# Weight splits as own programs, memory projections one pass earlier, and buffers lent between stages, in a one-core hybrid attention layer

## The chip, the core and the metric

The kernel runs on one core of a Trainium2 chip. Its time is device time in microseconds (us), the median of several runs. Five engines matter: TensorE (PE in the rows; PEld is its weight load), VectorE (DVE), ScalarE (ACT), GpSimd (POOL) and SyncE (SP), which issues every DMA here from one queue, in order.

## The reference, cut to what matters

One decoder layer over 2048 tokens of width 1024: a normalised input `h`, one wide projection, three groups of heads, gates, an output projection.

```python
h = rmsnorm(x, pre_g)
proj = h @ w_in          # sb_q k v gate | dsa_q ckv gate | idx_q idx_k idx_w | mem_q mem_gate
sb = stick_breaking_attention(sb_q, sb_k, sb_v)            # 6 heads
ds = dsa_sparse_attention(dsa_q, rmsnorm(dsa_ckv, kv_g), w_uk, w_uv,
                          idx_q, idx_k, idx_w, rel_bias, topk=256)   # 6 heads, indexer + top-k
mem_k, mem_v = split(mem @ w_mem_kv, 2)                    # 256 memory tokens
mo = softmax(mem_q @ mem_k.T / 8) @ mem_v                  # 4 heads
y = concat([sb * silu(sb_gate), ds * silu(dsa_gate), mo * silu(mem_gate)]) @ w_out
return x + rmsnorm(y, post_g)
```

## The kernel before

Every product with the input or with weights is done in three fp32r matmuls: each operand is split into a rounded part `hi` and a rest `lo`, and `three` (line 973) issues hi·hi, hi·lo and lo·hi.

The kernel is written as small programs (Python generators: an operation is yielded, a buffer is asked for with `Alloc`, another program's result with `Need`). A planner (`Plan.run`, line 518) runs them when the kernel is built: it keeps simulated times of the engines, holds a fixed number of programs of each queue open, and at each step issues the operation that could start first, by its own prices (`price`, line 346; a matmul of n columns costs n/2.216 ns). What comes out is one fixed instruction order for each engine, and one fixed order of DMAs on SP. All instructions go out of line 501, so the rows below tell them apart by their tiles, not by lines.

Three queues start together: `main`, the projections (9 programs open, window of 48 operations); `index`, the indexer with its top-k search for token blocks 2 to 15; `sb`, 48 stick-breaking programs of 256 queries and one head. `low` and `high` (the sparse and the memory heads) start from `STARTS`: `low` when `index` and `sb` have ended.

`main` makes three passes over 512-token chunks, in the order of `SEGMENTS`: pass 0 takes chunks 0 and 1 (indexer and latent projections alone), pass 1 chunks 2 and 3 with all units, pass 2 chunks 0 and 1 with the remaining units. A unit (`t_unit`, line 989) is 128 output columns: it splits its weights into two pairs of tiles (`wsplit`, line 948: DMA to `wr`, cast to `wth`, difference to `wtl`), then does 24 matmuls of 512 columns for each chunk, and evicts. `turn` makes the units split their weights in the order of the list. `"g4+g5"` is two units whose chunks alternate.

`hprep` (line 830) makes a chunk's `H`: for each of 8 row blocks it asks for an `hh` and an `hl` buffer, loads 256 KB of `xT` into an `xh` buffer, multiplies by the norm (DVE, two SBUF operands), rounds (ACT or DVE), and takes the difference (POOL or DVE). There are 16 `hh` and 16 `hl` buffers, that is two chunks; a new chunk waits until a chunk of the pass before is done. `xh` has 2 buffers (group `G`), and `ev` buffers may stand in.

`mem_kv` (line 1187) projects the memory tokens. It stands first in pass 2, splits the memory input into `hh` and `hl` buffers, and `hprep` of pass 2 waits for it (line 835).

SBUF is cut into groups (`LAYOUT`, line 1839); `HANDOVER` re-cuts a group into other buffers when named stages have passed and its old buffers are free. `LENT` lets one kind of buffer stand in for another. `R` holds 4 pairs of weight buffers. `S` and `T` belong to `sb`; `dQ`, a sparse or memory head's queries (512 KB), has 2 buffers (lines 1880 and 1881).

A memory head (`mem`, line 1733) does four 128-query blocks, each with its own PSUM bank, maximum, negation and `softmax` (line 1635), whose last operation is a reciprocal of one column. Sparse heads call `softmax` too. `pair_out` (line 1651) scales two heads' outputs by those reciprocals.

Of the kernel before, what the change touches and what calls it, by code (L numbers as in the profile page):

```python
# [11 lines left out]
F32 = mybir.dt.float32  # L12
# [4 lines left out]
AF = mybir.ActivationFunctionType  # L17
OP = mybir.AluOpType
# [93 lines left out]
class Eng:  # L112
# [18 lines left out]
MEMB = "pz"  # L131
# [436 lines left out]
class Net:  # L568
# [185 lines left out]
    def attention(self):  # L754
# [15 lines left out]
        blocks = [4 * g + j for g in gs for j in range(4)]  # L770
        return {"low": (low, *QUEUES["low"], lambda: self.stage("low")),
# [13 lines left out]
    def segment(self, seg, half):  # L785
# [12 lines left out]
        made = {"wa": lambda: self.nat_w("a", half, seg == 0), "wb": lambda: self.nat_w("b", half), "late": self.late_consts,  # L798
                "memkv": self.mem_kv, "near": self.near_bias, "through": self.nat_through}
# [7 lines left out]
        for name in SEGMENTS[seg].split():  # L807
# [22 lines left out]
    def hprep(self, seg, c):  # L830
# [3 lines left out]
        if seg == 2:  # L834
            yield Need("mem")
        yield Written([("RB", c)])
        rb = None
        for kt in range(8):
            hi = yield Alloc("hh", [P, 512], F32R)
            lo = yield Alloc("hl", [P, 512], F32R)  # L840
            H.append((hi, lo))
            if rb is None:
                rb = yield Alloc("ev", [P, 512], F32)
                yield pl.sp.dma_start(rb, self.RB[c], rt=[("RB", c)], prio=-1)
            xt = yield Alloc("xh", [P, 512], F32)
            yield pl.sp.dma_start(xt, a["xT"][kt * P:(kt + 1) * P, cs], prio=-1)
# [5 lines left out]
        pl.objs["H", seg, c] = H  # L852

# [135 lines left out]
    def t_unit(self, seg, cs, *units):  # L989
        pl = self.pl  # L990
        U = []
        mine = yield from self.turn()
        for unit, fn, u, *args in units:
# [5 lines left out]
            U.append((W, tiles, fn, u, args))  # L999
        pl.objs["begun unit", mine] = True  # L1000
        held = []
        for c in cs:
            H = yield Need(("H", seg, c))
            for W, tiles, fn, u, args in U:
# [142 lines left out]
    def nat_b(self, seg, c):  # L1147
# [15 lines left out]
        if c % 2:  # L1163
            pl.F(*tiles)

# [21 lines left out]
    def mem_kv(self):  # L1187
        pl, a = self.pl, self.a
        mine = yield from self.turn()
        M, held = [], []  # L1190
        for k in range(0, 8, 2):
            hi, lo = yield from self.wsplit(a["memT"][:, k:k + 2, :], 2, 256, "hh", "hl")
            M += [(hi[:, j, :], lo[:, j, :]) for j in range(2)]
            held += [hi, lo]
        pl.objs["mem"] = True
        for u in range(2):
            W, tiles = [], []
            for k in range(0, 8, 4):
                wh, wl = yield from self.wsplit(a["wmk"][u][:, k:k + 4, :], 4, P, "wth", "wtl")
                tiles += [wh, wl]  # L1200
                W += [(wh[:, j, :], wl[:, j, :]) for j in range(4)]
            ps = yield Alloc(MEMB, [P, 512], F32)
            for kt in range(8):
                yield from self.three(ps[:, :256], W[kt], M[kt], kt, 8)
# [8 lines left out]
        ps = None  # L1213
        for k in range(0, 8, 2):
            wh, wl = yield from self.wsplit(a["wmv"][:, k:k + 2, :], 2, 256, "wth", "wtl")
            if ps is None:
                ps = []
                for t in range(2):
                    ps.append((yield Alloc(MEMB, [P, 512], F32)))
            for t in range(2):  # L1220
                ts = slice(t * P, (t + 1) * P)
                for j in range(2):
                    m = (M[k + j][0][:, ts], M[k + j][1][:, ts])
                    yield from self.three(ps[t][:, :256], m, (wh[:, j, :], wl[:, j, :]), k + j, 8)
            pl.F(wh, wl)
# [767 lines left out]
```

## Time and profile before

| | us |
|---|---|
| median of 3 runs | 1467.66 (1462.12 to 1468.32) |
| the profiled execution | 1466.34 |
| its span, first to last instruction | 1464.5 |

All views of the profile come from that one execution. In the views by window, a row of a window gives, after the window and its length, the busy us of each engine (with the number of instructions), then the granted TensorE clock as a share of 2.4 GHz, the mean busy share of the 16 DMA engines, and GB/s. In the views by group, `out<-in` are tile names: `pp`, `pz`, `pT` and `po` are PSUM banks, and other single letters are the groups of SBUF.

### The profile page before, as it was taken

How to read it: one execution, taken by the hardware profiler on the slowest of the kernel's cores; microseconds unless marked ns; L12 is line 12 of the kernel's file. 1: busy time of each engine (PE TensorE's matmuls, PEld its weight loads, DVE VectorE, ACT ScalarE, POOL GpSimd, SP SyncE). 2: the span in 40 equal slices, each digit the busy share in tenths (PEclk: the TensorE clock that was granted, in tenths of full speed). 3: DMA queues.
4: the chain of work that ended last, by engine and by line, in shares of the span. 5: the costliest groups of instructions: out<-in, count | busy, mean ns of one | idle time of the engine just before them, and what ended most of it. 6: DMA issues, size and time to landing. Idle time of an engine off the chain costs nothing.

```text
span 1464.5 us, 25363 instructions
## 1 busy us (share of the span) xinstructions
PE 1372.6 (94%) x7662; PEld 1157.0 (79%) x7662; DVE 1159.1 (79%) x3467; ACT 969.8 (66%) x2147; POOL 497.2 (34%) x689
## 2 busy tenths in 40 slices
PE   7778999999999879999999999788999999999997
PEld 5656788877777567988888887677988989898885
DVE  6368888989998978998877677878987899998332
ACT  6556666767776777877777568766856666656221
POOL 5454222322213553135355440453323121202342
PEclk9879999999999899999999999989999999999998
DMA  7484485677424557467798375977575463643452
GB/s 276 138 235 135 145 249 162 183 205 200 129 88 143 163 169 229 147 188 220 217 266 250 104 249 173 294 228 214 166 235 166 151 205 100 181 123 87 137 174 95
DMA packets 222783, 264.28 MB, mean 180 GB/s; under 512 B 17670, under 2 KB 141996, under 8 KB 222636
## 3 DMA queue, kind: packets, MB, share of 16 engines
q1 hardware_dynamic: 222636, 262.56, 59.4%
q8 instruction: 63, 1.03, 0.3%
q14 instruction: 84, 0.69, 0.1%
HBM read 183.58 MB, written 78.91 MB: 179 GB/s over the span
## 4 chain that ended last, share of the span: by engine, by line
PE 68%; DVE 14%; ACT 7%; DMA 6%; issue 3%; POOL 1%; SPq 1%; DVEq 0%; ACTq 0%; POOLq 0%
PE pp L501 37%; PE po L501 11%; PE pz L501 10%; PE pT L501 10%; DVE A L501 5%; DVE D L501 2%; DVE E L501 2%; DVE K L501 2%; DMA B<-qd 1%; ACT J L501 1%; ACT E L501 1%; DMA kd<-E 1%; ACT B L501 1%; SPq L501 1%; DVE B L501 1%
## 5 line engine op out<-in xcount | busy, mean ns | idle before, releaser
L501 PE MATMUL pp<-H,R 128*128 128x512 f32 x2520 | 685.1, 403 | 15.5 <-ACT H L501 8.3
L501 PEld LDWEIGHTS pp<-H,R 128*128 128x128 f32 x2520 | 461.1, 190 | 103.8 <-ACT H L501 8.7
L501 POOL TENSOR_TENSOR R<-Q,R 128x512 fp32r<-128x512 f32 x92 | 119.3, 1300 | 246.4 <-DVE R L501 98.1
L501 ACT ACTIVATE pz<-pz 128x512 f32<-128x512 f32 (+3 forms) x221 | 111.1, 512 | 13.6 <-PE pz L501 12.7
L501 PE MATMUL po<-K,B 128*128 128x256 f32 (+3 forms) x386 | 95.7, 312 | 4.3 <-DVE A L501 1.9
L501 PE MATMUL pp<-W,H 128*128 128x296 f32 (+1 forms) x448 | 93.0, 298 | 1.0 <-ACT H L501 0.7
L501 POOL TENSOR_TENSOR V<-S,U 128x256 f32<-128x256 bf16 x48 | 32.7, 682 | 176.0 <-DVE C L501 149.5
L501 ACT ACTIVATE J<-A,D 128x384 uint8<-128x384 f32 (+9 forms) x60 | 75.5, 1258 | 23.3 <-DVE D L501 23.1
L501 ACT ACTIVATE E<-pp 128x512 f32<-128x512 f32 (+2 forms) x85 | 48.3, 568 | 54.2 <-PE pp L501 47.4
L501 ACT CAST K<-pT 128x512 fp32r<-128x512 f32 (+3 forms) x126 | 61.3, 493 | 32.9 <-PE pT L501 29.1
L501 PEld LDWEIGHTS po<-K,B 128*128 128x128 f32 x386 | 66.4, 191 | 19.1 <-DVE A L501 6.8
L501 PE MATMUL pT<-pack,T 128*128 128x128 f32 x334 | 78.3, 277 | 0.4 <-DVE K L501 0.3
L501 PE MATMUL pp<-V,H 128*128 128x296 f32 (+1 forms) x320 | 74.4, 307 | 1.8 <-DVE D L501 1.1
L501 PEld LDWEIGHTS pp<-W,H 128*128 128x128 f32 x448 | 72.8, 195 | 2.0 <-ACT H L501 0.9
L501 PE MATMUL pz<-H,R 128*128 128x512 f32 x192 | 63.6, 421 | 4.1 <-DVE C L501 2.2
L501 PEld LDWEIGHTS pp<-V,H 128*128 128x128 f32 x320 | 57.6, 202 | 3.8 <-DVE E L501 1.7
L501 POOL TENSOR_TENSOR V<-A,U 128x256 f32<-128x256 bf16 (+1 forms) x48 | 31.0, 653 | 80.9 <-DVE C L501 78.5
L501 DVE TENSOR_TENSOR K<-pT,K 128x512 fp32r<-128x512 f32 (+3 forms) x88 | 49.8, 571 | 10.4 <-ACT K L501 7.9
L501 PE MATMUL pz<-K,B 128*128 128x512 f32 (+3 forms) x138 | 53.2, 401 | 4.4 <-DVE A L501 2.9
L501 POOL TENSOR_TENSOR T<-T 128x384 f32<-128x384 f32 (+2 forms) x38 | 31.5, 829 | 70.8 <-DVE D L501 30.0
L501 ACT ACTIVATE po<-po 128x512 f32<-128x512 f32 (+3 forms) x87 | 45.0, 530 | 15.8 <-PE po L501 15.3
L501 DVE SCALAR_TENSOR_TENSOR A<-pz,iw,A 128x512 f32<-128x512 f32 (+3 forms) x82 | 53.4, 652 | 2.4 <-ACT pT L501 0.4
(476 smaller groups left out, 3796.8 us busy)
## 6 DMA issues: line engine op xcount, KB each, us to landing
Q<-wt SPq DMA_DIRECT2D x84, 256.0 KB, 4.3
B<-qd SPq DMA_DIRECT2D x24, 512.0 KB, 5.4
B<-vd SPq DMA_DIRECT2D x33, 256.0 KB, 3.7
gt<-E SPq DMA_DIRECT2D x32, 256.0 KB, 3.2
B<-qm SPq DMA_DIRECT2D x16, 512.0 KB, 5.0
S<-qsb SPq DMA_DIRECT2D x29, 256.0 KB, 5.0
S<-vsb SPq DMA_DIRECT2D x29, 256.0 KB, 4.5
B<-iq SPq DMA_DIRECT2D x56, 128.0 KB, 3.9
```

Source lines behind the costliest of these rows:

```text
L501: o.fn(*o.args, **o.kw)
```

## The change

- `t_unit` is cut in two: `t_weights` splits the weights (and takes the turn), `t_unit` waits for them and multiplies. `xload` is a program that loads a chunk's `xT` tiles; it stands ahead of `hprep`, which now waits for a tile before it asks for `hh` and `hl`. `main` holds 12 programs open.
- The memory projections move from the head of pass 2 into pass 1, in parts: `memin` (input split, into `mm` buffers cut from groups V and W, which the row-layout weights have left), `mw0` to `mw3` (weights), `memkv` (matmuls, now in the PSUM banks `pp`).
- The last four units of pass 1 run as one combined unit, so that all four finish chunk 2 before chunk 3; in pass 2, `q0+k0` and `q1+k1` are combined.
- Group T, which `sb` uses later, holds 4 `xh` buffers until pass 1 has its input; U lends 3 until pass 2 has its own; `ev` no longer stands in. V and W hold 4 more pairs of weight buffers after `memkv`. After `sb`, S holds `dQ`, `mV`, `mK` and `dK` buffers until the 16 memory heads are done, and only then the masks.
- `softmax` no longer takes the reciprocal; `pair_out` takes it once for 8 columns. A memory head puts two query blocks into one bank, with one maximum and one negation for both.
- There are more of the smallest buffers (`sm`, `mx`, `rl`).

```diff
-MEMB = "pz"
+MEMB = "pp"
...
-    "h0 wa a0 h1 i0 i1 a1 kv0 kv1 near q0 k0 wb b0 b1 q1 k1 q2 k2 d1 d0 d2 m0 g2 m1 g0 g1 g3 g4+g5 g6+g7",
-    "memkv h0 h1 q0 k0 q1 k1 wb b0 b1 q2 k2 through d1 d0 d2 m0 m1 g0 g1 g2 g3 g5 g4 g6+g7",
+    "h0 wa a0 h1 i0 i1 a1 kv0 kv1 near q0 k0 wb b0 b1 q1 k1 q2 k2 d1 d0 d2 m0 g2 m1 memin mw0 g0 mw1 memkv g1 mw2 mw3 g3 g4+g5+g6+g7",
+    "h0 h1 q0+k0 q1+k1 wb b0 b1 q2 k2 through d1 d0 d2 m0 m1 g0 g1 g2 g3 g5 g4 g6+g7",
...
         for name in names:
             if name in made:
+                if name[0] == "h" and seg:
+                    out.append(self.xload(seg, cs[int(name[1])]))
                 out.append(made[name]())
...
+                out.append(self.t_weights(seg, name == last, *[unit[n] for n in us]))
                 out.append(self.t_unit(seg, cs, *[unit[n] for n in us]))
...
-        if seg == 2:
-            yield Need("mem")
         yield Written([("RB", c)])
         rb = None
         for kt in range(8):
+            if rb is None:
+                rb = yield Alloc("ev", [P, 512], F32)
+                yield pl.sp.dma_start(rb, self.RB[c], rt=[("RB", c)], prio=-1)
+            xt = yield Need(("xt", seg, c, kt))
             hi = yield Alloc("hh", [P, 512], F32R)
             lo = yield Alloc("hl", [P, 512], F32R)
...
+    def xload(self, seg, c):
+        pl = self.pl
+        for kt in range(8):
+            xt = yield Alloc("xh", [P, 512], F32)
+            yield pl.sp.dma_start(xt, self.a["xT"][kt * P:(kt + 1) * P, c * 512:(c + 1) * 512], prio=-1)
+            pl.objs["xt", seg, c, kt] = xt
...
+    def t_weights(self, seg, last, *units):
         mine = yield from self.turn()
...
+            pl.objs["W", seg, unit] = (W, tiles)
         pl.objs["begun unit", mine] = True
+        if last:
+            self.stage(f"seg{seg}")
...
+    def t_unit(self, seg, cs, *units):
         for c in cs:
             H = yield Need(("H", seg, c))
+            for unit, fn, u, *args in units:
+                W, tiles = yield Need(("W", seg, unit))
...
+    def mem_in(self):
+        for k in range(0, 8, 2):
+            hi, lo = yield from self.wsplit(self.a["memT"][:, k:k + 2, :], 2, 256, "mm", "mm")
...
+    def mem_w(self, n):
+        mine = yield from self.turn()
...
     def mem_kv(self):
         for u in range(2):
+            W, tiles = yield Need(("mw", u))
...
+        V = []
+        for n in (2, 3):
+            w = yield Need(("mw", n))
+            V.append(w)
         for t in range(2):
+            ps = yield Alloc(MEMB, [P, 512], F32)
+            for kt in range(8):
+                m = (self.M[kt][0][:, ts], self.M[kt][1][:, ts])
+                yield from self.three(ps[:, :256], m, V[kt // 4][0][kt % 4], kt, 8)
+            if t:
+                pl.F(*V[0][1], *V[1][1], *self.Mt)
+                self.stage("memkv")
...
-        yield pl.dve.reciprocal(l, l)
...
+        yield pl.dve.reciprocal(L, L)
...
-        for j in range(4):
+        for s in range(2):
             ps = yield Alloc("pz", [P, 512], F32)
...
+            yield pl.dve.tensor_reduce(mx[:, 0:2], ps.rearrange("p (a b) -> p a b", a=2), axis=AX.X, op=OP.max)
+            yield pl.dve.tensor_scalar(mx[:, 2:4], mx[:, 0:2], -1.0, None, op0=OP.mult)
...
+        self.mems += 1
+        if self.mems == 16:
+            self.stage("mem")
...
-    "S": [("sQ", 512, 2), ("sK", 512, 2), ("sV", 512, 3), ("sx", 256, 4)],
-    "T": [("s0", 385, 2), ("s1", 384, 3), ("s2", 256, 1)],
+    "S": [("wth", 512, 4), ("wtl", 512, 4), ("", 512, 1)],
+    "T": [("xh", 512, 4), ("", 144, 1)],
...
+    ({"seg0"}, "S", [("sQ", 512, 2), ("sK", 512, 2), ("sV", 512, 3), ("sx", 256, 4)]),
+    ({"nat1"}, "V", [("mm", 512, 2)]),
+    ({"nat1"}, "W", [("mm", 512, 7)]),
+    ({"memkv"}, "V", [("wth", 512, 1), ("wtl", 512, 1)]),
+    ({"memkv"}, "W", [("wth", 512, 3), ("wtl", 512, 3)]),
+    ({"seg1"}, "V", [("wnh", 296, 5)]),
+    ({"seg1"}, "W", [("wnh", 296, 3), ("wnl", 296, 8), ("", 328, 1)]),
+    ({"h1"}, "T", [("s0", 385, 2), ("s1", 384, 3), ("s2", 256, 1)]),
+    ({"kv"}, "U", [("xh", 512, 3)]),
+    ({"kv", "h2"}, "U", [("s0", 385, 2), ("s1", 384, 1), ("s2", 256, 1)]),
+    ({"kv", "h2"}, "G", [("sQ", 512, 1), ("sK", 512, 1)]),
...
-    ({"sb"}, "S", [("mask", 1024, 4), ("yo", 512, 1)]),
+    ({"sb"}, "S", [("dQ", 1024, 2), ("mV", 256, 4), ("mK", 256, 2), ("dK", 512, 2)]),
+    ({"sb", "mem"}, "S", [("mask", 1024, 4), ("yo", 512, 1)]),
...
-QUEUES = {"main": (9, 3, 48), "index": (6, 0, 12), "sb": (8, 1, 16), "low": (12, 1, 32), "high": (8, 1, 16),
+QUEUES = {"main": (12, 3, 48), "index": (6, 0, 12), "sb": (8, 1, 16), "low": (12, 1, 32), "high": (8, 1, 16),
```

## Rows read from the trace of the kernel before

**Rows 1.** The page: busy us, share of the span, instructions.

```profile
PE 1372.6 (94%) x7662; PEld 1157.0 (79%) x7662; DVE 1159.1 (79%) x3467; ACT 969.8 (66%) x2147; POOL 497.2 (34%) x689
```

**Rows 2.** Windows, by stage: busy us of each engine, clock, DMA share, GB/s.

```profile
0.00:60.00 60.00, 44.20 (x210) 37.71 (x211) 31.73 (x55) 37.17 (x85) 31.02 (x29) 0.91 0.63 218
60.00:180.00 120.00, 98.83 (x512) 81.14 (x511) 88.80 (x297) 72.71 (x200) 48.45 (x48) 0.90 0.58 171
180.00:480.00 300.00, 297.22 (x1445) 240.57 (x1446) 268.41 (x833) 215.67 (x448) 75.61 (x110) 1.00 0.58 170
480.00:545.00 65.00, 50.38 (x227) 37.79 (x226) 55.26 (x108) 48.19 (x95) 39.20 (x35) 0.87 0.60 169
545.00:840.00 295.00, 292.98 (x1706) 252.28 (x1705) 246.48 (x608) 219.45 (x507) 121.18 (x272) 1.00 0.69 202
905.00:1010.00 105.00, 86.10 (x486) 70.67 (x484) 78.78 (x276) 75.91 (x221) 43.41 (x38) 0.90 0.82 255
1010.00:1350.00 340.00, 334.55 (x2239) 297.77 (x2238) 304.72 (x1037) 226.21 (x408) 79.73 (x98) 1.00 0.52 158
```

**Rows 3.** Instructions on tensor xT: issues, first and last start.

```profile
L501 SPq DMA_DIRECT2D E<-xT x20: 327/379/561, 91.0 to 539.7; - x20
L501 SPq DMA_DIRECT2D G<-xT x12: 328/388/758, 84.1 to 138.5; - x12
...
DMA to landing us min/median/max: 2.7/4.6/6.8
```

**Rows 4.** Groups by shape: an H tile's product (DVE), and its difference (POOL).

```profile
L501 DVE SCALAR_TENSOR_TENSOR E<-E,pack,E 128x512 f32<-128x512 f32 x20 | 16.3, 817 | 5.2 <-DMA E<-xT 5.2
L501 POOL TENSOR_TENSOR H<-E,H 128x512 fp32r<-128x512 f32 x20 | 27.4, 1379 | 24.8 <-ACT H L501 17.5 <-DVE D L501 5.2 <-PE pp L501 2.0
```

**Rows 5.** Timeline of DVE around 83 us: two casts of one form.

```profile
82.59 0.42 DVE L501 CAST R<-Q 128x512 fp32r<-128x512 f32 x1
...
83.15 1.51 DVE L501 CAST R<-Q 128x512 fp32r<-128x512 f32 x1
```

**Rows 6.** Timeline of POOL in the same stretch.

```profile
83.09 1.29 POOL L501 TENSOR_TENSOR R<-Q,R 128x512 fp32r<-128x512 f32 x1 [9.26 <-DVE R L501]
```

**Rows 7.** Timeline of PE, 466 to 545 us; brackets: idle before, and releaser.

```profile
465.77 11.00 PE L501 MATMUL pp<-H,R 128*128 128x512 f32 x47
...
520.80 0.73 PE L501 MATMUL pp<-H,R 128*128 128x512 f32 x2 [1.96 <-ACT R L501]
524.36 1.43 PE L501 MATMUL po<-R,H 128*128 128x256 f32 x5 [2.83 <-POOL R L501]
```

**Rows 8.** Windows: a part of the stretch 905 to 1010 us.

```profile
925.00:955.00 30.00, 23.83 (x138) 18.92 (x138) 23.19 (x79) 23.93 (x74) 16.75 (x14) 0.89 1.05 344
```

**Rows 9.** Instructions on tensors qm, msk and qsb: loads, first and last start.

```profile
L501 SPq DMA_DIRECT2D B<-qm x16: 524/525/622, 864.4 to 986.1; - x16
...
L501 SPq DMA_DIRECT2D A<-msk x8: 422/430/653, 840.5 to 941.4; - x8
L501 SPq DMA_DIRECT2D S<-msk x8: 319/402/507, 1067.4 to 1195.9; - x8
...
L501 SPq DMA_DIRECT2D A<-qsb x8: 557/584/1356, 735.1 to 791.0; - x8
```

**Rows 10.** Groups by shape: VectorE's small operations of the softmaxes.

```profile
L501 DVE RECIPROCAL C<-C 128x1 f32<-128x1 f32 x160 | 25.4, 159 | 25.0 <-ACT T L501 9.2 <-ACT A L501 7.8 <-ACT W L501 3.5
L501 DVE TENSOR_SCALAR C<-C 128x1 f32<-128x1 f32 x176 | 25.6, 151 | 1.7
L501 DVE TENSOR_REDUCE C<-pz 128x1 f32<-128x256 f32 x25 | 10.1, 414 | 1.5 <-PE pz L501 1.4
L501 DVE CUSTOM_DVE_ANT_0 T<-pz,S 128x512 f32<-128x512 f32 x19 | 12.9, 685 | 1.6 <-PE pz L501 1.5
```

**Rows 11.** What SP's DMA queue waited for, 36 to 140 us.

```profile
SPq L501 <- DVE E L501: 28.2, 13, 4.5
SPq L501 <- POOL H L501: 7.9, 7, 2.7
```

More of the change, by code (lines that the diff above doesn't have):

```diff
@@ L798, in segment @@
         made = {"wa": lambda: self.nat_w("a", half, seg == 0), "wb": lambda: self.nat_w("b", half), "late": self.late_consts,
-                "memkv": self.mem_kv, "near": self.near_bias, "through": self.nat_through}
+                "memkv": self.mem_kv, "memin": self.mem_in, "near": self.near_bias, "through": self.nat_through}
+        for n in range(4):
+            made[f"mw{n}"] = lambda n=n: self.mem_w(n)
         for k, c in enumerate(cs):
@@ L806, in segment @@
         out, uses = [], 0
-        for name in SEGMENTS[seg].split():
+        names = SEGMENTS[seg].split()
+        last = [n for n in names if n not in made][-1]
+        for name in names:
             if name in made:
+                if name[0] == "h" and seg:
+                    out.append(self.xload(seg, cs[int(name[1])]))
                 out.append(made[name]())
@@ L1164, in nat_b @@
             pl.F(*tiles)
+        if seg == 1 and c % 2:
+            self.stage("nat1")
     def kv_chunk(self, c):
@@ L1185, in kv_chunk, with mem_kv @@
             self.stage("kv")
-    def mem_kv(self):
+    def mem_in(self):
+        pl = self.pl
+        self.M, self.Mt = [], []
+        for k in range(0, 8, 2):
+            hi, lo = yield from self.wsplit(self.a["memT"][:, k:k + 2, :], 2, 256, "mm", "mm")
+            self.M += [(hi[:, j, :], lo[:, j, :]) for j in range(2)]
+            self.Mt += [hi, lo]
+    def mem_w(self, n):
         pl, a = self.pl, self.a
         mine = yield from self.turn()
[L1190 to L1195, printed above, removed]
-        for u in range(2):
[L1197 to L1201, printed above, removed]
+        W, tiles = [], []
+        for k in range(2):
+            if n < 2:
+                hi, lo = yield from self.wsplit(a["wmk"][n][:, 4 * k:4 * k + 4, :], 4, P, "wth", "wtl")
+                W += [(hi[:, j, :], lo[:, j, :]) for j in range(4)]
+            else:
+                kt = 4 * (n - 2) + 2 * k
+                hi, lo = yield from self.wsplit(a["wmv"][:, kt:kt + 2, :], 2, 256, "wth", "wtl")
+                W += [(hi[:, j, :], lo[:, j, :]) for j in range(2)]
+            tiles += [hi, lo]
+        pl.objs["mw", n] = (W, tiles)
+        pl.objs["begun unit", mine] = True
+    def mem_kv(self):
+        pl = self.pl
+        for u in range(2):
+            W, tiles = yield Need(("mw", u))
             ps = yield Alloc(MEMB, [P, 512], F32)
             for kt in range(8):
-                yield from self.three(ps[:, :256], W[kt], M[kt], kt, 8)
+                yield from self.three(ps[:, :256], W[kt], self.M[kt], kt, 8)
             pl.F(*tiles)
@@ L1212, in mem_kv @@
             pl.F(e)
[L1213 to L1225, printed above, removed]
-        pl.objs["begun unit", mine] = True
-        for t in range(2):
-            yield from self.ev_v(ps[t][:, :256], 4, self.VM[t * P:(t + 1) * P, :, :], ("VM", t))
-            pl.F(ps[t])
-        pl.F(*held)
+        V = []
+        for n in (2, 3):
+            w = yield Need(("mw", n))
+            V.append(w)
+        for t in range(2):
+            ts = slice(t * P, (t + 1) * P)
+            ps = yield Alloc(MEMB, [P, 512], F32)
[5 more added lines that the diff above has]
+                self.stage("memkv")
+            yield from self.ev_v(ps[:, :256], 4, self.VM[t * P:(t + 1) * P, :, :], ("VM", t))
+            pl.F(ps)
     def iq_load(self, i, iqS, rt):
```

37 lines of the change are left out of this document (17 added, 20 removed).

## Prediction

> **What bounds the kernel now.** I read the busy shares first, then the windows by stage, then, in the stages that lose time, the instructions on one tensor, the groups by shape and the timelines. The reader is to see that TensorE is the busiest engine over the span, 94% against VectorE's 79% [rows 1], and that its idle time is not spread out. Of 1372.6 us busy in a span of 1464.5 us, 91.9 us are idle: 15.8 in the first 60 us, 21.2 from 60 to 180, 14.6 from 480 to 545, 18.9 from 905 to 1010, and only 2.8 from 180 to 480, 2.0 from 545 to 840 and 5.5 from 1010 to 1350 [rows 2]. So a change gains where a pass is handed to the next (60 to 180, 480 to 545) and where the memory and sparse heads start after the projections (905 to 1010), and hardly elsewhere.
>
> Idle time is not the whole loss. The granted clock is 1.00 in the full stages and 0.90, 0.87 and 0.90 in the three poor ones [rows 2]: part of each ran at the lower level, 1.2 of 2.4 GHz. I put the loss of a stage between its idle time and that plus the whole clock deficit: 60 to 180, 21.2 to 33.2 us (0.10 x 120 more); 480 to 545, 14.6 to 23.1 (0.13 x 65); 905 to 1010, 18.9 to 29.4 (0.10 x 105).
>
> **First handover, x loads and H.** The 16 xT tiles of pass 1 are loaded from 84.1 to 138.5 us [rows 3]. The last still has to land (4.6), be multiplied (0.82) and rounded and subtracted (1.38, plus a cast I take at 0.6) [rows 3, 4]: some 62 us for 16 tiles, 3.9 each. A tile's own work is far shorter: POOL's difference, the longest step, takes 1.38, so the loop is held by its two or three x buffers, each of which waits for a load and a whole conversion. The change loads six tiles (2 in G, 4 in T) before H buffers come free, out of the 0.42 of the DMA engines that 60 to 180 leaves unused [rows 2]. Then 16 tiles take from 16 x 1.38 = 22 us (POOL alone) to 16 x (0.82 + 1.38) = 35 us (both steps in turn), which releases 27 to 40 us of the conversion. TensorE can win back at most its loss, 21.2 to 33.2. VectorE has the room: 88.8 of 120 busy. But the row-layout weights of pass 1 still have to be split after pass 0's, and the indexer's chains run as before, so some loss stays. Value taken: 20; ends: 5 (a rival below) and 33.
>
> **Second handover.** Pass 2 now begins with the memory projections: they take hh and hl buffers, hprep waits for them, and TensorE waits for their splits (1.96 and 2.83 us before two groups, released by ACT's and POOL's work on R [rows 7]). After the change their matmuls run inside pass 1, which is full; their number is the same, so they cost there what they cost here. Chunk 2's H comes free after the last four units have used it, and chunk 3 of these four, 4 x 24 matmuls of 0.234 (47 in 11.00 us [rows 7]), is 22.5 us of cover. Eight tiles of the next chunk need 8 x 2.20 = 17.6 us, five of them loaded ahead (2 in G, 3 in U), so they fit. If that cover were gone, the price would be the 17.6 us. What is late next is the weights of q0+k0, whose buffers are held until the combined unit has ended: two casts and two differences, about 2 x (0.42 + 1.29) = 3.4 us [rows 5, 6], and less where indexer matmuls fill in. The stage loses up to 23.1 now; I take 18 as won (23.1 less 3.4, less 1.7 for a half filled start). Ends: 8, and 23.
>
> **Start of the memory and sparse heads.** The 16 query loads of memory heads are issued from 864.4 to 986.1 us [rows 9], one in 8.1 us with other heads between, on two dQ buffers that the sparse heads use as well. S gives two more, with K and V buffers, so that twice as many heads overlap. The DMA engines are 0.82 busy from 905 to 1010 [rows 2]; the free 0.18 x 105 = 18.9 us bounds what faster loading can save. Value taken: 14; ends: 0 (a rival below) and 18.9. The masks of the last token groups now wait for S until the memory heads are done. The first S<-msk load stands at 1067.4, 81 us after the last memory query load [rows 9]: that distance hides it; without it, the wait for a load.
>
> **Softmax.** 160 reciprocals of 0.159 us, 25.4 us, with 25.0 us of VectorE idle before them, since each stands in VectorE's order behind its exponential on ACT [rows 10]. In their place come 20 of eight columns (12 sparse and 8 memory pairs), between 0.16 and 0.41 each by the nearest rows: 3 to 8 us. In the memory heads 64 maxima of 0.414 become 32 over 512 columns (about 0.685, the nearest PSUM read of that width): 26.5 to 21.9 us; 64 negations become 32, 4.8 us less [rows 10]. VectorE is relieved of 27 to 32 us busy and up to 25 idle. But TensorE idles only 5.5 us in 1010 to 1350 [rows 2], so this is worth 0 to 5.5 there; I take 2. What it does from 905 to 1010 is in the 14.
>
> **What costs.** In pass 1 the projection of memory values holds all four R pairs until its last matmul, so the next unit's weights are split after it: 0.42 + 1.29 for the first pair, some 2 us; the window of 12 and the finer programs also reorder everything a little. I take 3 lost, ends 0 and 8. The bank `pp` for `pz`, the larger small buffers and T's late return cost nothing: the cover of the last is that `sb` in pass 1 has only a few programs to run, and from 545 to 840, where `sb` does most of its work, T, U and G are its own again. If they were not, the 284 us of `sb` would be stretched.
>
> **Sum.** 20 + 18 + 14 + 2 - 3 = 51 us off the profiled execution's 1466.3, that is 1415; the median of the runs stands 1.3 higher, so 1416. A difference under 0.5%, 7.3 us, is about what a measurement of this kernel can't tell from none.
>
> **Rivals.**
>
> *The shared port holds the first handover* (1431). A cast of one form took 0.42 us at 82.59 and 1.51 at 83.15, while POOL ran a difference from 83.09 for 1.29 [rows 5, 6]: the two engines wait for each other. If every step from SBUF to SBUF of both engines goes in turn, the 35 us of H, eight splits of row-layout weights and two units' weights (12 x 1.71 = 21 at most) make 56 of the 62 us, and 5 is won in place of 20. The Trainium skill's page "SBUF — State Buffer", section "Who interferes with whom", has this as a rule: one port pair is shared by VectorE and GpSimd and locked for a whole instruction, and who comes second blocks. By that rule the time is this rival's; the long cast agrees with it. Against it: ACT can take the casts, and VectorE was only 74% busy in the stage.
>
> *The heads' start is bound by DMA* (1430). From 925 to 955 the 16 engines' share is 1.05 at 344 GB/s [rows 8], with the output weights loading at the same time. Then more buffers only queue more loads, and the 14 go. The page "DMA: Bandwidth & Descriptors", section "Where 436 GB/s comes from", in the Trainium skill puts the HBM limit of a core near 358 GB/s: the row agrees that this stretch is near it. Against the rival: the whole stage stands at 0.82 and 255 GB/s [rows 2].
>
> *The heads start no earlier* (1452). `low` begins when `sb` ends: the first mask loads at 840.5, and `sb` still loads queries at 791 [rows 9]. If `sb` were paced by its own buffers, `main` would end earlier and leave TensorE unfed until 840; 14 is left. Against it: TensorE is full from 545 to 840 [rows 2].
>
> *SP's queue blocks* (1485, the other side). An xT load that waits for a buffer stands ahead of all other DMAs. The planner prices every matmul at full speed, while the clock was 0.90; where the chip is behind the plan, SP reaches a load before POOL has released the buffer, and stores, weights and indexer loads stand behind it. If each of four chunks blocks SP for its conversion, 4 x 17.6 = 70 us go, against 51 won: 1466 - 51 + 70. It decides from 13 us per chunk on. SP already waits 28.2 us for evictions and 7.9 for H from 36 to 140 [rows 11]; but no wait there was over 4.5 us.
>
> *Nothing moves* (1466): the planner reorders, and the gaps open elsewhere; VectorE at 268.4 of 300 us from 180 to 480 [rows 2] leaves little room for work deferred into it.
>
> **How the numbers follow.** Chances: forecast 0.52, port 0.12, DMA 0.11, late heads 0.08, SP 0.09, nothing 0.08. The first four are faster by over 0.5%: 0.83; same 0.08; slower 0.09. The forecast's own range is 1395 to 1440. The upper ends together are 33 + 23 + 19 + 5.5, 80 us, so 1386 is the low end; the high end, 1456, takes in the port, DMA and late-head cases and leaves out the last two, 0.17.
>
> **What would show it.** xT loads for pass 1 issued well before 84 us and all 16 H conversions over by about 115; the gap of 480 to 545 gone, with memory matmuls inside pass 1 and a clock near 1.00 there; memory query loads closer than 6 us apart; 20 reciprocals on tile C in place of 160, with little idle before them. The forecast is wrong if TensorE's idle time between 60 and 180 stays above 15 us, if a new gap opens where pass 2 starts, or if SP shows single waits over 10 us for H.

## The result, and the profile after

The kernel after takes 1446.17 us (median of 4 runs, 1443.93 to 1446.53) against 1467.66 (4 runs): the ratio is 0.9859, 95% interval 0.9833 to 0.9885. It is 21.5 us faster, where 51 were forecast. The profiled execution took 1445.82 us with a span of 1443.9.

The page of the kernel after, answering to [rows 1]:

```profile
PE 1362.4 (94%) x7662; PEld 1156.2 (80%) x7662; DVE 1148.7 (80%) x3246; ACT 965.0 (67%) x2160; POOL 500.7 (35%) x689
```

Its windows by stage, answering to [rows 2] (columns as there), with two more, 180 to 215 and 840 to 990:

```profile
60.00:180.00 120.00, 103.83 (x526) 84.64 (x525) 92.57 (x317) 75.13 (x200) 52.16 (x53) 0.94 0.55 160
180.00:215.00 35.00, 27.48 (x144) 24.10 (x143) 25.93 (x91) 20.82 (x54) 7.88 (x10) 0.90 0.64 191
480.00:545.00 65.00, 60.71 (x267) 47.71 (x267) 55.40 (x115) 49.34 (x104) 33.72 (x42) 0.97 0.63 190
545.00:840.00 295.00, 293.42 (x1705) 251.65 (x1704) 243.92 (x628) 219.57 (x500) 115.55 (x259) 1.00 0.64 188
840.00:990.00 150.00, 133.13 (x778) 108.51 (x777) 114.08 (x349) 119.01 (x345) 57.73 (x63) 0.93 0.80 253
905.00:1010.00 105.00, 90.40 (x546) 74.69 (x545) 85.42 (x253) 79.71 (x233) 47.80 (x47) 0.92 0.78 246
1010.00:1350.00 340.00, 334.87 (x2212) 298.54 (x2211) 288.73 (x877) 217.13 (x398) 75.32 (x89) 1.00 0.47 148
```

The same two windows of the kernel before:

```profile
180.00:215.00 35.00, 34.38 (x186) 28.75 (x187) 30.33 (x111) 24.53 (x61) 7.47 (x14) 1.00 0.82 240
840.00:990.00 150.00, 134.49 (x759) 111.57 (x758) 109.93 (x411) 112.16 (x307) 55.47 (x58) 0.93 0.74 234
```

TensorE's idle time falls from 21.2 to 16.2 us in 60 to 180 and from 14.6 to 4.3 in 480 to 545; a new gap of 7.5 stands in 180 to 215, where there was 0.6; 840 to 990 is no better, 16.9 against 15.5.

A window of fixed times mixes stages that have moved. So I also line kernels up by matmul work: each kernel's matmuls in order of issue, each counted with the time from its issue to the next where nothing holds it (0.231 us for 512 columns, 0.175 for 384, 0.136 for 296, 0.118 for 256, 0.112 for 128), make 1295.0 us in every kernel but for their order. The lead is how much sooner a kernel has done so much of it than the kernel before (us, profiled executions; the second column is when the kernel before is there):

```
work done       90    250    410    570    770    810    890   1250
before at    145.2  315.3  479.4  671.2  873.9  919.8 1034.7 1407.4
after          7.5   -0.3   -0.3   20.8   20.1   16.1   17.9   19.4
e1 rb own      9.8   14.2    8.0   36.3   36.4    6.3   14.5   15.4
e2 no x loans -5.4   -2.5   -1.8   18.7   19.8   17.1   19.7   18.2
e9 chunk 2    10.3   -5.1   -9.0   20.8   21.8   16.2   19.6   17.0
e10 chunk 3   12.4   13.8    9.9   37.5   37.0    0.9    7.6    7.3
e11 sb order   7.9   -0.1    0.7   29.5   27.8   22.0   30.3   30.6
e12 all        7.9   12.7   12.1   38.3   35.0   33.1   36.8   38.0
```

Other prices for the matmuls move a lead by about 1 us, and by up to 3 in the column 810, where TensorE stands idle in some kernels. The executions shown of e10 and e12 were 4.8 and 6.2 us longer than the medians of these kernels, so their last columns are low.

Read the row "after": 7.5 us are won by the first handover and given back by work 250; 20 are won at the second and kept; some 3 go again where the heads start. The whole gain is the second handover. The rest of this text is about the other two places.

**The first handover.** Issues on tensor xT, pass 1's loads among them (first and last start at the end of a line), answering to [rows 3]:

```profile
L501 SPq DMA_DIRECT2D G<-xT x13: 327/351/731, 33.7 to 506.4; - x13
L501 SPq DMA_DIRECT2D T<-xT x10: 327/328/432, 34.7 to 108.9; - x10
```

Loads of the norm factors, from the view of tensor rb:

```profile
L501 SPq DMA_DIRECT2D E<-rb x4: 382/424/439, 82.6 to 412.4; - x4
```

The same in the kernel before:

```profile
L501 SPq DMA_DIRECT2D E<-rb x4: 327/376/941, 83.1 to 507.4; - x4
```

The x loads start at 33.7 us instead of 84.1, but the first rb load stands at 82.6, half a us from where it was (83.1). Without rb no H product can be made. The differences on POOL, from the view of tile H from 60 to 170 us (min/median/max ns, first and last start), in the kernel after, then the first line of it in the kernel before:

```profile
L501 POOL TENSOR_TENSOR H<-T,H x10: 1279/1678/1747, 95.0 to 123.7; 128x512 fp32r<-128x512 f32 x10
L501 POOL TENSOR_TENSOR H<-G,H x6: 1274/1504/1815, 90.5 to 120.2; 128x512 fp32r<-128x512 f32 x6
```

```profile
L501 POOL TENSOR_TENSOR H<-G,H x12: 1260/1288/1736, 90.3 to 145.9; 128x512 fp32r<-128x512 f32 x12
```

And what TensorE waited for from 180 to 215 (us, times, longest):

```profile
PE pp L501 <- DVE E L501: 6.6, 2, 3.7
```

The last of the 16 differences starts at 123.7; before, it started at 145.9. What follows them stalls: from 180 to 215 projections wait for VectorE's work on buffers of E, into which it evicts.

**The heads.** Mask loads, memory query loads and gate stores (`gt<-E`, the last one ends the projections) of the kernel after, from the views of the three tensors, answering to [rows 9]; then the gate stores of the kernel before:

```profile
L501 SPq DMA_DIRECT2D A<-msk x8: 351/438/526, 834.3 to 926.0; - x8
...
L501 SPq DMA_DIRECT2D B<-qm x9: 524/525/525, 853.4 to 941.6; - x9
...
L501 SPq DMA_DIRECT2D gt<-E x32: 319/326/524, 374.9 to 892.7; - x32
```

```profile
L501 SPq DMA_DIRECT2D gt<-E x32: 319/327/1372, 373.4 to 918.7; - x32
```

The memory queries are loaded within 88 us, where they took 122 [rows 9]. But the projections end 26.0 us earlier and the heads start (first mask load) only 6.2 us earlier: less projection work is left to cover their start.

**Softmax.** The groups on tile C, answering to [rows 10]:

```profile
L501 DVE TENSOR_REDUCE C<-pz 128x2 f32<-128x512 f32 x17 | 11.5, 677 | 2.2 <-PE pz L501 2.1
...
L501 DVE RECIPROCAL C<-C 128x8 f32<-128x8 f32 x20 | 3.8, 191 | 0.0
```

**SP.** Its queue from 36 to 140 us, answering to [rows 11]:

```profile
SPq L501 <- DVE E L501: 25.3, 9, 6.9
SPq L501 <- POOL H L501: 11.0, 10, 1.6
```

### The profile page after: what moved, and what is told of

Its sections match the earlier page's. It is cut to its first block, busy times and chain, and to the rows that moved or that the text cites. A ratio compares the mean times of both kernels' runs of the same rounds, so it can differ in the third digit from the quotient of the medians.

```text
span 1443.9 us, 25133 instructions
## 1 busy us (share of the span) xinstructions
PE 1362.4 (94%) x7662; PEld 1156.2 (80%) x7662; DVE 1148.7 (80%) x3246; ACT 965.0 (67%) x2160; POOL 500.7 (35%) x689
## 3 DMA queue, kind: packets, MB, share of 16 engines
q8 instruction: 63, 1.03, 0.3%
## 4 chain that ended last, share of the span: by engine, by line
PE 72%; ACT 5%; DVE 5%; DMA 2%; issue 2%; POOL 1%; SPq 0%; ACTq 0%; POOLq 0%; DVEq 0%
PE pp L501 40%; PE po L501 12%; PE pz L501 10%; PE pT L501 9%; DVE K L501 1%; ACT A L501 1%; ACT T L501 1%; DVE C L501 1%; DVE A L501 1%; DVE E L501 1%; DMA Q<-wt 1%; DMA kd<-E 1%; ACT K L501 1%; ACT V L501 0%; POOL H L501 0%
## 5 line engine op out<-in xcount | busy, mean ns | idle before, releaser
L501 PE MATMUL pp<-H,R 128*128 128x512 f32 x2448 | 675.4, 403 | 20.0 <-ACT H L501 7.7
L501 PEld LDWEIGHTS pp<-H,R 128*128 128x128 f32 x2448 | 446.4, 190 | 105.1 <-ACT H L501 8.7
L501 POOL TENSOR_TENSOR R<-Q,R 128x512 fp32r<-128x512 f32 x84 | 109.2, 1304 | 219.5 <-PE pp L501 40.0
L501 PE MATMUL po<-K,B 128*128 128x256 f32 (+3 forms) x357 | 89.6, 311 | 3.0 <-ACT K L501 1.2
L501 ACT ACTIVATE J<-A,D 128x384 uint8<-128x384 f32 (+9 forms) x60 | 75.5, 1258 | 16.3 <-DVE D L501 15.8
L501 PEld LDWEIGHTS po<-K,B 128*128 128x128 f32 x357 | 60.3, 189 | 13.6 <-DVE A L501 2.4
L501 ACT CAST K<-pT 128x512 fp32r<-128x512 f32 (+3 forms) x106 | 55.1, 526 | 21.7 <-PE pT L501 15.1
L501 DVE SCALAR_TENSOR_TENSOR A<-pz,iw,A 128x512 f32<-128x512 f32 (+3 forms) x102 | 67.1, 657 | 3.1 <-DVE A L501 0.5
L501 POOL TENSOR_TENSOR R<-E,R 128x512 fp32r<-128x512 f32 x26 | 33.5, 1289 | 82.3 <-ACT R L501 79.9
L501 DVE TENSOR_TENSOR E<-pp,E 128x512 f32<-128x512 f32 (+3 forms) x76 | 43.3, 571 | 13.9 <-ACT E L501 13.4
L501 DVE TENSOR_SCALAR D<-D 128x1 uint8<-128x1 f32 (+1 forms) x308 | 42.2, 163 | 15.0 <-ACT J L501 11.1
```

What stands on the lines that cost most here:

```text
L501: o.fn(*o.args, **o.kw)
```

## Experiments

All times are medians of 4 runs; the ratio is to the kernel before on the same chip. The kernel after stands at 0.9859 (0.9833 to 0.9885).

**e1: own buffers for the norm factors**

```diff
-    "T": [("xh", 512, 4), ("", 144, 1)],
+    "T": [("xh", 512, 2), ("rbx", 512, 2), ("", 144, 1)],
...
-                rb = yield Alloc("ev", [P, 512], F32)
+                rb = yield Alloc("rbx" if seg == 1 else "ev", [P, 512], F32)
```

> Two of the four x buffers that T lends in pass 1 become two buffers for the norm factors (rb), so that the conversion of a chunk's H no longer has to get one of the four `ev` buffers, which the row-layout evictions use too. Theory 1: the start of the first handover's conversion is set by the wait for an `ev` buffer (the rb load was issued at 82.6 us in the kernel after, and the first H product stood at 88.2), and the stall that stands at 180 to 215 us (TensorE 27.5 of 35 us busy) is the same `ev` buffers' scarcity, put off. Then the rb load comes before 75 us, the last H difference on POOL before 115 (after: 123.7), TensorE's idle time from 180 to 215 falls from 7.5 to under 3 us, and the time to about 1436 (8 to 12 us under 1446). Theory 2: VectorE and POOL pace the conversion by taking turns (16 tiles in 37 us); then the start may be earlier but the 16 tiles still take 35 us or more, the gain is lost again by 215 us, and the time stays within 4 us of 1446. Theory 3, x loads as the prediction had it: two x buffers fewer make the conversion later, and the time 5 to 10 us longer.

Measured: 1448.3 us, ratio 0.9868 (0.9837 to 0.9898). Two of its windows:

```profile
180.00:215.00 35.00, 34.60 (x247) 32.70 (x247) 32.32 (x115) 23.22 (x51) 6.80 (x10) 1.00 0.64 197
...
840.00:885.00 45.00, 34.51 (x147) 27.03 (x146) 24.35 (x96) 21.19 (x57) 21.69 (x27) 0.73 0.92 290
```

Its row-layout stores from 100 to 220 us, and those of the kernel after in the same stretch, from the view of tensor vsb:

```profile
L501 SPq DMA_DIRECT2D vsb<-E x16: 319/320/762, 114.5 to 214.2; - x16
```

```profile
L501 SPq DMA_DIRECT2D vsb<-E x8: 319/326/1994, 131.8 to 216.7; - x8
```

The end of e1's projections and the start of its heads (gate stores, mask loads):

```profile
L501 SPq DMA_DIRECT2D gt<-E x32: 314/326/1297, 351.1 to 850.5; - x32
```

```profile
L501 SPq DMA_DIRECT2D A<-msk x8: 422/431/1427, 839.8 to 936.0; - x8
```

Theory 1 held at its place and failed in the total. The gap of 180 to 215 is gone, twice as many row-layout stores are issued from 100 to 220, and the lead is 14.2 at work 250 and 36 at 570 to 770. Then 30 us of it go within 40 us of work: at 840 the projections are at their end (last gate store 850.5), the heads start at 839.8 (first mask load), and TensorE is busy 34.5 of 45 us at a granted clock of 0.73, that is partly at the lower level, having idled. One expectation missed: the last difference did not come before 115 but at 123.3, although the conversion began at 75.0.

**e9 and e10: which of the two buffers**

```diff
-                rb = yield Alloc("rbx" if seg == 1 else "ev", [P, 512], F32)
+                rb = yield Alloc("rbx" if (seg, c) == (1, 2) else "ev", [P, 512], F32)    # e9; (1, 3) in e10
```

> As e1, but only chunk 2's norm factors (the first conversion) have a buffer of their own; chunk 3's take an `ev` buffer as in the kernel after. Reading a: what e1 won at the first handover (13 us, all of it still there at 400 us) came from the earlier start of the conversion (75.1 us against 90.5); then this run has it too, TensorE's idle time from 180 to 215 is under 2 us (after: 7.5), and TensorE stands 8 us or more ahead of the kernel before at 250 us. Reading b: it came from the `ev` buffer that chunk 3's factors hold while the row-layout evictions want all four; then the start is at 75 here too, but the stall from 180 to 215 stays over 5 us, and nothing is won at 250.

> The other half of e1: only chunk 3's norm factors have a buffer of their own, chunk 2's wait for `ev` as in the kernel after. Reading a: the conversion starts at 88 to 90 us as in the kernel after, and the stall from 180 to 215 stays. Reading b: that stall falls under 2 us, and TensorE stands 8 us or more ahead at 250 us, although the conversion starts no earlier. By either reading the total is 1444 to 1450, since what is won is lost at 840 where the heads wait for the last stick-breaking program.

Measured: e9 1447.17 us, 0.9858 (0.9834 to 0.9882); e10 1453.0 us, 0.9899 (0.9876 to 0.9922). The window 180 to 215, e9 first:

```profile
180.00:215.00 35.00, 29.70 (x115) 22.71 (x114) 28.88 (x92) 23.33 (x56) 10.65 (x16) 0.85 0.62 176
```

```profile
180.00:215.00 35.00, 32.66 (x182) 27.73 (x181) 31.13 (x113) 23.22 (x56) 13.22 (x23) 1.00 0.78 224
```

The differences on POOL in e10:

```profile
L501 POOL TENSOR_TENSOR H<-G,H x8: 1277/1502/1825, 87.8 to 123.1; 128x512 fp32r<-128x512 f32 x8
L501 POOL TENSOR_TENSOR H<-T,H x8: 1269/1289/1656, 91.0 to 127.4; 128x512 fp32r<-128x512 f32 x8
```

Reading b. e9's first difference on POOL is at 75.5 us, and it stands 5.1 us behind at work 250; e10's is at 87.8, 2.7 before the kernel after, its last later (127.4), and it stands 13.8 ahead. What holds the first handover is the `ev` buffer that chunk 3's factors keep while the row-layout evictions need it, not when the conversion starts. (e10's gap is 2.3 us, not under 2.) The total of e10 is 3 us over what was expected: the larger lead meets the same wall at 840.

**e2: the x loans undone**

```diff
-    "T": [("xh", 512, 4), ("", 144, 1)],
+    "T": [("s0", 385, 2), ("s1", 384, 3), ("s2", 256, 1)],
...
-    ({"kv"}, "U", [("xh", 512, 3)]),
```

(S also goes to the stick-breaking heads from the start.)

> The loans ahead of and around the passes are undone: T and S belong to the stick-breaking heads from the start, U lends no x buffers; x has its two buffers in G, the programs and their order stay as in the kernel after. Prediction's step: the first handover was held by x buffers, so without the loan the last H difference moves from 123.7 us back to about 140, and the 7 us that the kernel after has won by 140 us are gone; since they were lost again by 215, the time is 1446 to 1456. Theory 1 (the `ev` buffer for rb gates the start, and what is won is lost by 215): the conversion ends later, but the time stays within 4 us of 1446. For the second handover the prediction had five x tiles loaded ahead (2 in G, 3 in U); if they matter there, TensorE idles 8 us or more from 480 to 545 (after: 4.3), and the time is 1452 to 1460.

Measured: 1446.55 us, 0.9861 (0.9841 to 0.9881); the window 480 to 545:

```profile
480.00:545.00 65.00, 59.03 (x277) 47.76 (x276) 58.31 (x127) 49.66 (x99) 33.45 (x40) 0.95 0.63 185
```

The differences on POOL:

```profile
L501 POOL TENSOR_TENSOR H<-G,H x16: 1265/1290/1625, 90.1 to 157.3; 128x512 fp32r<-128x512 f32 x16
```

The last one starts at 157.3 instead of 123.7 us, later than the 140 expected. So the loans do make the conversion 34 us shorter. A lead of 7.5 at work 90 becomes -5.4, but at 250 the two kernels stand within 3 us, and the total does not move. For the time the loans of x buffers are worth nothing here, at either handover (idle 6.0 against 4.3 in 480 to 545).

**e5 and e6: where the memory projections stand, and the combined units**

```diff
-... m1 memin mw0 g0 mw1 memkv g1 mw2 mw3 g3 g4+g5+g6+g7"
+... m1 g0 g1 g3 g4+g5 g6+g7"
-    "h0 h1 q0+k0 q1+k1 wb ..."
+    "memin mw0 mw1 memkv mw2 mw3 h0 h1 q0+k0 q1+k1 wb ..."   # e5
...
-... g3 g4+g5+g6+g7"                                    # e6
+... g3 g4+g5 g6+g7"
-    "h0 h1 q0+k0 q1+k1 wb ..."
+    "h0 h1 q0 k0 q1 k1 wb ..."
```

(In e5, V and W also wait for `memkv` before they are cut for pass 2's row-layout weights.)

> The memory projections stand at the head of pass 2 again, with their own input buffers (mm), so that the conversion of pass 2's H does not wait for them; the last four units of pass 1 are two pairs instead of one group of four (the run with units apart is the control for that). Theory 1: their place costs, because TensorE waits there for their weight splits while chunk 2's units have run out: TensorE's idle time from 480 to 545 rises from 4.3 to 10 us or more, and the time is 1456 to 1462. Theory 2: what cost in the kernel before was that pass 2's conversion waited for them and they sat in its hh and hl buffers; with buffers of their own the place does not matter: idle time 480 to 545 under 7 us, the time within 5 us of the control.

> Pass 1 ends with g4+g5 and g6+g7 instead of one group of four, and pass 2 begins with q0, k0, q1, k1 one by one, as before; all else as in the kernel after. The prediction: the group of four gives 22.5 us of cover for the conversion of pass 2's first H, two pairs give 11.2 after chunk 2 is released, against 17.6 needed. If that step is right, the idle time from 480 to 545 rises from 4.3 us by about 6, and the time to 1450 to 1456. If other work fills in (the indexer, the stick-breaking heads), the idle time stays under 6 and the time within 4 us of 1446.

Measured: e5 1458.48 us, 0.9953 (0.9935 to 0.9971); e6 1450.05 us, 0.9895 (0.9877 to 0.9913). Window 480 to 545 in e5:

```profile
480.00:545.00 65.00, 57.17 (x275) 45.48 (x274) 53.93 (x117) 49.22 (x93) 36.13 (x41) 0.95 0.63 185
```

What TensorE waited for in e5 from 470 to 560 us:

```profile
PE pp L501 <- POOL R L501: 2.4, 1, 2.4
PE pp L501 <- ACT R L501: 2.0, 3, 1.4
```

The window in e6:

```profile
480.00:545.00 65.00, 60.83 (x272) 47.04 (x271) 53.62 (x104) 48.15 (x102) 38.25 (x46) 0.95 0.72 203
```

Against e6, e5 loses 0.0058 of the time, 8.5 us, although pass 2's conversion no longer waited for the memory projections: theory 1, at 7.8 us of idle time rather than 10, with the waits for weight splits (R) that [rows 7] show. But e5 and e6 differ in more than the place and pass 2's first units. V and W lend their four pairs of weight buffers once the memory projections are done, so in e5 they come too late for pass 1: in the kernel after and in e6, 120 matmuls of pass 1 have their weights there, in e5 none. The 8.5 us belong to the place and to these buffers together; what the place alone is worth is not shown. The group of four is not the cover that I took it for: apart, the idle time at the handover is 4.2 us against 4.3. What e6 loses in all (0.0036, 5.3 us, the intervals just overlapping) it does not lose there: its lead at work 490 is 20.4 us against 19.6, and TensorE's busy time from 840 to 885 is 42.4 against 44.6.

**e3 and e4: the heads' start**

```diff
-    "wout": {"main"},
+    "wout": {"main", "mem"},                                            # e3
...
-    ({"sb"}, "S", [("dQ", 1024, 2), ("mV", 256, 4), ("mK", 256, 2), ("dK", 512, 2)]),
-    ({"sb", "mem"}, "S", [("mask", 1024, 4), ("yo", 512, 1)]),
+    ({"sb"}, "S", [("mask", 1024, 4), ("yo", 512, 1)]),                 # e4
```

> The 16 loads of output weights (256 KB each, 4.2 MB), which start at 893 us when the projections end, start only when the 16 memory heads are done. Theory A (the heads' start is bound by DMA: 342 GB/s and a share of 1.03 from 900 to 940 us): 4.2 MB at 342 GB/s are 12.3 us of DMA time that leave the stretch; the share from 900 to 940 falls under 0.95, TensorE's idle time from 885 to 990 falls from 16.5 to under 9 us, and the time to 1434 to 1440. Theory B (the heads' start is held by buffers and by the chain of each head: maximum, exponential, split): the idle time stays over 13 us and the time within 4 us of 1446. Theory C: the output blocks miss their weights, and 1450 or more.

> S goes to the masks right after the stick-breaking heads, as before, and lends no query, key or value buffers to the memory heads. The prediction's step (more buffers start the heads faster, 14 us): the memory query loads spread from 88 us to about 120 again, TensorE's idle time from 885 to 990 rises from 16.5 to 25 or more, and the time to 1455 to 1460. Theory A (bound by DMA) and theory B's chain alike: the loads spread, but the idle time stays within 3 us of 16.5 and the time within 4 us of 1446.

Measured: e3 1443.19 us, 0.9845 (0.9813 to 0.9877); e4 1453.31 us, 0.9909 (0.9889 to 0.9929). Windows in the kernel after, then in e3:

```profile
885.00:990.00 105.00, 88.50 (x515) 71.96 (x514) 81.88 (x235) 83.60 (x255) 45.12 (x43) 0.90 0.78 246
900.00:940.00 40.00, 30.31 (x186) 24.36 (x184) 32.44 (x81) 31.27 (x102) 20.87 (x18) 0.92 1.03 342
```

```profile
885.00:990.00 105.00, 88.78 (x569) 73.28 (x568) 90.52 (x265) 90.19 (x267) 32.10 (x35) 0.97 0.74 230
900.00:940.00 40.00, 31.50 (x213) 25.73 (x211) 33.77 (x88) 33.17 (x113) 7.67 (x8) 1.00 0.86 263
```

The longest wait of TensorE's weight loads from 885 to 990, in the kernel after, then in e3:

```profile
PEld po L501 <- ACT K L501: 6.5, 10, 1.6
```

```profile
PEld po L501 <- ACT K L501: 6.4, 12, 1.3
```

Taking 4.2 MB out of the stretch lowers the DMA share from 1.03 to 0.86 and lifts the clock from 0.92 to 1.00, but TensorE's idle time from 885 to 990 stays (16.2 against 16.5), and so does the wait for ACT's rounding of the transposed exponentials (K). DMA is busy there without being the bound; of theory B's chain, this wait is the part that shows. The total's gain is inside the intervals. In e4 the loads spread over 116 us again, the idle time rises to 24.1, and 7 us are lost (idle time and total both 1 to 2 us short of what was expected): S's loan is worth half of the 14 that I gave it.

**e7 and e11: the order of the stick-breaking programs**

```diff
-            order = [(g, h) for g in (5, 6, 7, 0, 1, 2, 3, 4) for h in range(2)]
-            order += [(g, h) for g in (5, 6, 7, 0, 1, 2, 3, 4) for h in range(2, 6)]
+            order = [(g, h) for g in (5, 6, 7) for h in range(2)] + [(g, h) for g in (5, 6, 7) for h in range(2, 6)]
+            order += [(g, h) for g in (0, 1, 2, 3, 4) for h in range(2)] + [(g, h) for g in (0, 1, 2, 3, 4) for h in range(2, 6)]
```

> The kernel of e1 (own buffers for rb) with one more edit: the 48 stick-breaking programs are listed so that the 18 of token groups 5 to 7 (pass 1's chunks) all stand ahead of those that need pass 2's queries; now 6 of them are followed by 10 that wait for pass 2, and 8 are open at a time. Theory S: in e1 the gain of the first handover (13 us, and 36 us at 450 to 770) is lost at 840 because the heads start when the last stick-breaking program ends (first mask load 839.8 us, after 834.3, before 840.5), which no change moved; if the list frees them earlier, the first mask load comes at 825 or before, TensorE's idle time from 840 to 885 falls from 10.5 to under 5 us, and the time to 1430 to 1440. Rival: they are paced by their own chain and buffers after pass 2's queries have come, so that the mask load stays at 835 to 842, and the time at 1444 to 1450.

> The kernel after with the order of the stick-breaking programs of e7 alone. If the heads' start is worth something by itself, the first mask load comes at 826 or before (after: 834.3) and the time is 1437 to 1443; if e7's gain needs the first handover's, since VectorE has no room for these programs in pass 1, the mask load moves by less than 4 us and the time stays within 4 us of 1446.

Measured: e7 1434.26 us, 0.9796 (0.9775 to 0.9817); e11 1433.0 us, 0.9769 (0.9734 to 0.9804). Mask loads in e7, then in e11:

```profile
L501 SPq DMA_DIRECT2D A<-msk x8: 423/431/1524, 821.9 to 914.6; - x8
```

```profile
L501 SPq DMA_DIRECT2D A<-msk x8: 320/434/1192, 826.4 to 917.9; - x8
```

Theory S. The first mask load had stood between 832 and 847 us in every run, whatever the projections did; it moves with the list alone, and the time with it, by 13 us (e11: 0.0090 of 1466). (In e11 the load came 0.4 us later than expected and the time 4 us lower.) Not all of the 13 us are won at the heads. A window of e11:

```profile
480.00:545.00 65.00, 64.88 (x313) 52.13 (x312) 58.12 (x126) 50.06 (x109) 43.89 (x51) 1.00 0.67 192
```

TensorE idles 0.1 us there instead of 4.3, and 9 us more of lead stand at work 570 already (29.5 against 20.8). What the list does at the heads is plainer from e7 and e1: between work 770 and 890, e1 loses 22 us of lead and e7 7. What e1 adds to the total is not to be measured (e7 and e11 overlap): in e7 TensorE still idles 7.9 us from 840 to 885, where I expected under 5.

**e12: together**

e1, the order of e7, the output weights of e3, and 12 stick-breaking programs open instead of 8.

> All that helped together: own buffers for rb, the new order of the stick-breaking programs with 12 open instead of 8, and the output weights after the memory heads. If the gains add (e7 stands 12 us under the kernel after, e3 3 us), the time is 1424 to 1432, the first mask load at 815 or before, and TensorE's idle time from 840 to 990 under 18 us (after: 16.9; e7: 22.5). If the stretch after the last stick-breaking program has another limit (DMA, or the chain in a head), it stays at 1432 to 1437.

Measured: 1421.45 us, 0.968 (0.9648 to 0.9712). Mask loads (tensor msk):

```profile
L501 SPq DMA_DIRECT2D A<-msk x8: 422/432/1472, 809.6 to 903.6; - x8
```

The window 840 to 990:

```profile
840.00:990.00 150.00, 133.12 (x855) 111.17 (x853) 125.22 (x374) 129.24 (x359) 45.16 (x50) 0.98 0.75 232
```

It beats both kernels, by 46 and 25 us. The heads start 24.7 us earlier than in the kernel after. The idle time of 840 to 990 is 16.9 us as there, at a clock of 0.98 instead of 0.93. The time is 3 us under the range expected; what the 12 open programs give by themselves was not tried.

**e8: the softmax part undone**

```diff
         yield pl.act.activation(E, src, AF.Exp, bias=nm, accum_out=l)
+        yield pl.dve.reciprocal(l, l)
...
-        yield pl.dve.reciprocal(L, L)
```

(Also a memory head's four banks, maxima and negations, as before.)

> The softmax part alone is undone: a reciprocal of one column in each softmax, and four banks, maxima and negations in a memory head. Prediction's term: 2 us (0 to 5.5), since TensorE idles only 5 us from 1010 to 1350; then the time is 1446 to 1452, with VectorE 25 to 30 us busier. Rival: the chain of a head (maximum, exponential, reciprocal) is what TensorE waits for from 885 to 990, where its idle time is 16.5 us; then that rises to over 20 and the time to 1453 or more.

Measured: 1449.51 us, 0.9892 (0.9873 to 0.9911), 4.8 us by the ratios, with overlapping intervals. The group of reciprocals in e8:

```profile
L501 DVE RECIPROCAL C<-C 128x1 f32<-128x1 f32 x160 | 25.0, 158 | 12.3 <-ACT A L501 5.3 <-ACT T L501 2.6 <-ACT W L501 2.2
```

The idle time from 885 to 990 is 14.5 us, so the rival falls. VectorE is 8.5 us busier over the span (1157.2), not 25 to 30. Summed one by one, its instructions take 22.0 us more (1363.9 against 1341.8): records of neighbouring instructions overlap, and the busy time counts an overlap once.

## Why the prediction was half right

**Second handover: right, and its size too.** 18 forecast, 20 measured in the lead. Of the reasons, the memory projections' place holds, together with the weight buffers that it sets free (8.5 us by e5 against e6); the 22.5 us of cover from the combined unit (e6) and the five x tiles loaded ahead (e2) do not matter. How the other 11 us divide among conversion, weight programs and the wider window was not tried, so that the size came out is in part luck.

**First handover: 20 forecast, nothing kept.** The failed step is "TensorE can win back at most its loss", with 20 taken: it counts what the conversion of H releases as time that TensorE gets. The conversion did become shorter by the x loads: the last of its 16 differences starts at 123.7 us instead of 145.9 (and at 157.3 without the loans, e2), and from the first product on it took 37 us, where 22 to 35 were forecast. But by work 250 TensorE had nothing of it, because the evictions after it stalled at 180. The runs showed another shortage in its place, in `ev`, the buffers that rb, the row-layout's raw values and its evictions share. Of the 13 changed kernels, the four in which chunk 3's factors have a buffer of their own (e1, e7, e10, e12) lead by 13 to 17 us at work 250. The nine others stand between 5 us behind and 1 ahead, whether their last difference starts at 121 us or at 157. I looked at xT alone; rb is the other input of the same product, its load stood at 83.1 us just before the first xT load at 84.1, and the step gave it no wait. That wait set the start, but an earlier start won nothing either (75.5 us in e9). My sign "xT loads for pass 1 issued well before 84 us" came true and meant nothing; "idle time between 60 and 180 stays above 15 us", the sign of failure, came true as well (16.2).

**Heads' start: 14 forecast, about -3.** The step "twice as many heads overlap" was carried out (loads within 88 us) and is worth 7 us (e4). What failed is that I counted it against an unchanged start. The projections end 26 us earlier, the heads only 6, and the cover between is lost. The rival "the heads start no earlier" named this mechanism, with a chance of 0.08 and a condition that was too strict: I argued against it from TensorE being full from 545 to 840. It was full, of projections, and so ran out of them.

**Softmax: 2 forecast, about 5** by e8, whose interval overlaps with that of the kernel after. The reciprocal of eight columns took 0.191 us, near the low bound. The negations were mis-sized: one of two columns took 0.242 us, not the 0.151 of one column, so halving their number saved VectorE about 1.5 us and not 4.8.

```profile
L501 DVE TENSOR_SCALAR C<-C 128x2 f32<-128x2 f32 x32 | 6.8, 242 | 0.2
```

**What costs: 3 forecast.** The leads show no separate loss at 250 to 410 (-0.3), where the memory projections and their weights are added.

**Rivals.** SP's queue did not block from 36 to 140 us: its longest wait was 6.9 us, and for H 1.6. The port rule bore itself out and did not decide. The 16 H products of pass 1 took 1.30 us on average (1.43 in the ten T buffers, 1.08 in the six G buffers), against 0.94 in pass 1 before; the 0.82 of [rows 4] is mostly pass 2. Products that no operation of POOL overlapped took 0.73 to 0.75 us in both kernels, the others up to 1.87. POOL's differences took 1.56 us on the T tiles, and 1.28 on the tiles Q late in the kernel:

```profile
L501 DVE SCALAR_TENSOR_TENSOR T<-T,pack,E 128x512 f32<-128x512 f32 x10 | 13.9, 1433 | 0.0
...
L501 POOL TENSOR_TENSOR H<-T,H 128x512 fp32r<-128x512 f32 x10 | 15.4, 1558 | 0.8 <-ACT H L501 0.7
L501 POOL TENSOR_TENSOR H<-Q,H 128x512 fp32r<-128x512 f32 x16 | 20.2, 1277 | 30.1 <-DVE H L501 22.3 <-DMA W<-kd 2.9 <-PE pp L501 2.8
```

The Trainium skill, page "SBUF — State Buffer", section "Who interferes with whom", has the two engines lock one port pair; these rows agree. But e10 wins its 13.8 us with a conversion that ends no earlier (127.4). The DMA rival is refuted as a bound by e3, although the stretch ran at a share of 1.03.

## What to carry to other kernels

Before making a loop faster with more of one buffer, ask what the next engine lacks when the loop ends sooner, and who else takes from the buffers of the loop's other inputs: here the shortage was in `ev`, not in x. Follow a gain to the next trigger: the 16 us that e1 had won over the kernel after by work 770 were lost at the queue that opens when the last stick-breaking program is done. A first-come list with a fixed number of open programs blocks on entries that cannot run yet, and putting the ones that can first took 13 us off, more than any one change of buffers tried here.

## What was unexpected of the hardware

A VectorE reciprocal of 8 columns took 191 ns and one of 1 column 158, but a negation of 2 columns 242 and one of 1 column 156: what more columns cost differs from one small operation to the next. In e1 TensorE idled 10.5 of the 45 us from 840 to 885, and the granted clock of that stretch was 0.73, a mean of both levels; in the kernel after, busy for 44.6 of them, it was 1.00:

```profile
840.00:885.00 45.00, 44.63 (x265) 36.55 (x264) 32.20 (x115) 35.41 (x91) 12.60 (x20) 1.00 0.86 269
```

By the matmul prices given with the leads, e1 did 20.5 us of work in that stretch and the kernel after 41.9. Of the 21.4 us between them the idle time accounts for 10; an estimate from these figures leaves 11 for the lower level, about as much again.
